# Six small moves in a one-core hybrid layer: where loads, copies and splits of weights stand in their queues

## The chip, the cores and the metric

The kernel runs on one core of one Trainium2 chip. The metric is the device time of one execution in microseconds (us), as the median of several. A profiled execution is a further one, with its own time; its span runs from the first to the last instruction.

A core has five engines, each with its own queue that is worked through in order: TensorE (PE; its weight loads are shown as PEld), VectorE (DVE), ScalarE (ACT), GpSimd (POOL) and SyncE (SP), which here only issues transfers (DMA). ScalarE issues some transfers too.

## The reference

One layer of a language model for 512 tokens of 1024 numbers, all in float32. In outline:

```python
h = rms_norm(x, norm_mix_pre)
z = h @ w_in                                   # 1024 -> 8016
o_a = rwkv7_time_mix(z[:, :3360], ...)         # 16 heads of 64, state recurrence, group norm, gate g = sigmoid(gd) @ g2
o_b = nsa_attention(z[:, 3360:5968], ...)      # 16 query heads in 4 groups: compressed, selected, window branch
g_a, g_b = split(sigmoid(z[:, 5968:]), 2)
m = g_a * (o_a @ w_branch_rwkv) + g_b * (o_b @ w_branch_nsa)
x = x + rms_norm(m @ w_out, norm_mix_post)
u = causal_dwconv(rms_norm(x, norm_ffn_pre) @ ffn_up, conv_w, conv_b)   # 1024 -> 2 x 2816
x = x + rms_norm((silu(u_gate) * u_val) @ ffn_down, norm_ffn_post)
```

With 512 tokens there are eight blocks of 64 keys and up to 16 may be selected, so the selected branch takes every block that is allowed. The window of 512 covers the whole sequence as well.

## The kernel before, in words

**Products in two halves.** To keep float32 accuracy on TensorE's reduced float32 format, each operand is split into a high part (a copy in that format) and a low part (what is left). A product is three matmuls: high with high, high with low, low with high (`mm3`, `proj_steps`). Activations are split once. Weights are split as they come: `split_to` loads a raw tile by SP, copies it to the high part on ScalarE (`act`, L124) and subtracts on GpSimd or VectorE for the low part (L162). `split_w` does so for the two halves of a block of 1024 x 128 weights. Raw, high and low tiles each stand in a ring of three buffers (`WB = 3`, tags `raw`, `whi`, `wlo`), so a load waits until a raw tile three loads back is split.

**Stages.** (1) Norm of x, transposed into `hh`, `hl`; low-rank projections. (2) RWKV in two groups of four head pairs: `inputs` projects k, r, v of a pair, `prep` computes decays and normalised keys, `couple` makes the chunk matrices, `invert` and `recur` solve and run the recurrence over eight chunks of 64, and `finish` normalises the group's output, adds the bonus (`bvl`), multiplies by the gate and writes to DRAM. (3) Attention in eight phases, one for each pair of heads p8: in a phase `values(p8)` (transposes and products with values) and `score(p8 + 1)` (scores, softmax) are woven together with projection work as filling. (4) The two branch projections and gates (`branch`). (5) The output projection by token tiles of 128 (`wo_tok`), residual and norm. (6) The gated MLP: `half_up` for the first `NU = 3` blocks of up-weights by halves of the tokens, then 41 whole blocks; (7) the down projection.

**What sets the order.** The code is written as Python generators. `drive` runs one filling generator and, in each round, advances the spawned threads by their rate (`FR = 0.5`: a step every second round). In the attention phases `steps` sorts the steps of all generators by a fraction of the phase. This gives the program order. A planner then lists the instructions anew: on each engine it takes, among those that by its own timing are ready, the first in program order. So an instruction that is ready early floats ahead, and one edit can reorder what follows. `tc.keep_in_program_order(i)` pins an instruction behind all that was traced before it on its engine; `late=True` does so for the high copy of a split. The order on an engine is then fixed, and the engine waits for whatever stands first.

**What the change touches.**

- `finish` (L824): for each pair it splits its gate weights g2 (L847), loads `bvl` (L850), and three steps later transposes the output to a bank `gt` of tag `px`, scales it, adds `bvl` (L866), and multiplies by the gate product `pg` (also `px`; L871 to L875). The first group's finish runs beside `prep` and `couple` of the second group, the second group's beside the attention's first phases.
- PSUM banks: tags `pj`, `px`, `py`, `pz`, two each. `prep` puts the squared norms of the keys into `pn` (L533), from which ScalarE (L536) and then GpSimd (`nte`, L544) make the factors that `pb`'s transposes (L562) need.
- `invert` has a scratch tile `TM` in pool `rh` (L642).
- `vcp` (L988 to L993): the compressed values, masked and split, on ScalarE and VectorE ahead of the attention; the first values phase reads them at L1154. `vload` (L996) loads and transposes the other values as a thread of its own.
- `qload` (L929) loads the four half tiles of a pair's queries; called at the start of phase p8 for pair p8 + 2.
- `norm` in `score` (L1051): scales the softmax numerators of both branches, on VectorE for branch b = 0 and on GpSimd for b = 1, but on VectorE for both in the first head of the first pair (L1061).
- `wo_load` (L1263): loads and splits output weights during the branch stage; the first `NW = 13` go to tiles of their own.
- The stretch between output projection and MLP (L1413 to L1426): `norm_x` and `norm_t` of token tiles 2 and 3 beside `half_up`.

## Time and profile before

| | |
|---|---|
| median of 3 runs | 1175.86 us (1175.56, 1175.86, 1177.87) |
| profiled execution, its own time | 1178.1 us |
| its span | 1176.3 us |
| TensorE busy | 1153.3 us, 98% of the span |
| VectorE, ScalarE, GpSimd busy | 580.7, 579.6, 581.4 us |
| mean clock granted to TensorE | 0.993 |
| transfers | 131.94 MB, mean 112 GB/s |

How to read it. A row of busy time by stage has the stretch in us from the span's start, its length, and for each engine its busy us with the number of instructions; then the clock granted to TensorE (1.00 is full), the share of the transfer engines and GB/s. A row of a timeline has start, duration, engine, line, operation, `out<-in`, shapes, and in brackets how long the engine stood before it and what ended that. A row of waits has the total in us, how often, and the longest. Matmuls are pipelined and their ends are modelled: on their own they are 0.39 us long in the timeline, though one starts about every 0.23 us.

### The profile page before, as it was taken

To read this page: it belongs to the slowest core of one execution; us is meant where nothing else is said; L and a number is where in the kernel's file an instruction comes from. 1 tells how busy PE (TensorE), PEld (TensorE's weight loads), DVE (VectorE), ACT (ScalarE), POOL (GpSimd) and SP (SyncE) were. 2 spreads that over 40 slices of the span, in tenths; PEclk is the share of its full clock that TensorE was granted. 3 is DMA by queue.
4 is the path that set the end of the run, shared out by engine and by line. 5 is a ranking of instruction groups with operands and counts; after the bars stand their busy time and mean duration, and the time that the engine had idled before them with its cause. 6 is when DMAs were issued, how large, how long until landed. Compare 5 with 4: busy or idle time off the path is not lost.

```text
span 1176.3 us, 19883 instructions
## 1 busy us (share of the span) xinstructions
PE 1153.3 (98%) x7414; PEld 923.4 (78%) x7414; DVE 580.7 (49%) x1208; ACT 579.6 (49%) x1149; POOL 581.4 (49%) x525
## 2 busy tenths in 40 slices
PE   8999999999999999999999999999999999999997
PEld 6888888877788887766767777788888888888886
DVE  4225555635555552678887757655433343331103
ACT  5536653544665434467776655443544444443311
POOL 4336664435576442456576553511555565554430
PEclk8999999999999999989999999999999999999999
DMA  6522335321343653233533126541223233334421
GB/s 226 133 81 74 88 101 169 108 82 42 107 140 100 190 178 122 78 99 125 178 105 95 54 64 210 180 160 45 72 90 101 97 99 99 98 92 138 129 63 72
DMA packets 95651, 131.94 MB, mean 112 GB/s; under 512 B 34178, under 2 KB 37058, under 8 KB 95299
## 3 DMA queue, kind: packets, MB, share of 16 engines
q1 hardware_dynamic: 79634, 116.26, 31.7%
q10 hardware_dynamic: 15920, 14.42, 3.9%
q8 instruction: 58, 0.95, 0.3%
q14 instruction: 39, 0.31, 0.1%
HBM read 108.30 MB, written 19.14 MB: 108 GB/s over the span
## 4 chain that ended last, share of the span: by engine, by line
PE 86%; DVE 5%; issue 3%; ACT 2%; POOL 2%; DMA 1%; SPq 0%; DVEq 0%; POOLq 0%; ACTq 0%
PE pu L222 6%; PE pu L221 6%; PE pu L223 6%; PE o L1134 4%; PE dn L1307 3%; PE dn L1308 3%; PE dn L1309 3%; PE pt L140 3%; PE gt L299 2%; PE gt L301 2%; PE gt L300 2%; PE ub L1191 2%; PE v L300 2%; PE v L299 2%; PE s L1078 2%
## 5 line engine op out<-in xcount | busy, mean ns | idle before, releaser
L1087 ACT ACTIVATE p<-p,stt 128x384 f32<-128x384 f32 (+3 forms) x128 | 70.7, 554 | 40.7 <-DVE stt L1085 39.3
L1449 DVE SCALAR_TENSOR_TENSOR u<-pu,cvec,u 128x511 f32<-128x511 f32 x44 | 33.0, 750 | 102.0 <-ACT u L1448 102.0
L1061 POOL TENSOR_SCALAR p<-p,stt 128x512 f32<-128x512 f32 (+3 forms) x60 | 68.4, 1151 | 26.7 <-DVE stt L1056 19.8
L1085 DVE CUSTOM_DVE_ANT_0 p<-s,rh 128x384 f32<-128x384 f32 (+3 forms) x128 | 59.3, 483 | 26.6 <-PE s L1071 17.8
L1453 POOL TENSOR_TENSOR u<-u,u 128x512 f32<-128x512 f32 x22 | 28.4, 1292 | 39.1 <-DVE u L1450 38.2
L140 PE MATMUL pt<-ident,p 128*128 128x128 f32 x320 | 45.5, 276 | 1.5 <-POOL p L1061 0.8
L1455 DVE TENSOR_TENSOR al<-u,ah 128x512 fp32r<-128x512 f32 x22 | 23.8, 1081 | 45.5 <-ACT ah L1454 45.5
L1134 PE MATMUL o<-PT,vt 128*64 128x256 f32 (+3 forms) x256 | 46.2, 452 | 0.0
L140 PEld LDWEIGHTS pt<-ident,p 128*128 128x128 f32 x320 | 38.0, 142 | 8.0 <-ACT p L1087 1.1
L1078 PE MATMUL s<-kst,qs 128*128 128x512 f32 (+1 forms) x128 | 38.4, 391 | 2.0 <-DVE stt L1085 2.0
L1448 ACT ACTIVATE u<-pu,cvec 128x512 f32<-128x512 f32 x44 | 33.6, 763 | 5.5 <-PE pu L1411 5.5
L1061 DVE TENSOR_SCALAR p<-p,stt 128x512 f32<-128x512 f32 (+3 forms) x68 | 35.4, 553 | 0.6
L1450 DVE SCALAR_TENSOR_TENSOR u<-pu,cvec,u 128x510 f32<-128x510 f32 x44 | 33.0, 749 | 1.6
L1134 PEld LDWEIGHTS o<-PT,vt 128*64 128x64 f32 x256 | 17.3, 139 | 19.6 <-issue 17.6
L1125 ACT ACTIVATE PT<-pt 128x512 f32<-128x512 f32 x48 | 27.5, 585 | 5.7 <-PE pt L140 5.6
L1078 PEld LDWEIGHTS s<-kst,qs 128*128 128x128 f32 x128 | 21.6, 191 | 10.9 <-DVE stt L1085 6.3
L1355 DVE TENSOR_TENSOR p2tm<-dn,gb 128x512 f32<-128x512 f32 x4 | 2.8, 692 | 51.2 <-ACT p2jl L1353 51.2
L1127 DVE COPY PT<-pt 128x512 f32<-128x512 f32 x32 | 21.9, 684 | 9.1 <-PE pt L140 9.0
L1454 ACT ACTIVATE ah<-u 128x512 fp32r<-128x512 f32 x22 | 13.9, 633 | 22.4 <-POOL u L1453 22.4
L804 ACT ACTIVATE UV<-xs 64x256 f32<-64x256 f32 x16 | 6.0, 378 | 37.5 <-PE xs L799 37.1
L1087 ACT ACTIVATION_READ_ACCUMULATOR p<-p,stt 128x1 f32 x128 | 24.1, 188 | 0.0
L657 DVE TENSOR_TENSOR XP<-XP,TM 128x30 f32<-128x30 f32 (+14 forms) x60 | 20.3, 338 | 2.0
(1758 smaller groups left out, 3943.9 us busy)
## 6 DMA issues: line engine op xcount, KB each, us to landing
gtd<-gt ACTq DMA_DIRECT2D x16, 256.0 KB, 2.6
qs<-qd SPq DMA_DIRECT2D x32, 128.0 KB, 3.1
g<-gtd SPq DMA_DIRECT2D x16, 256.0 KB, 3.3
xt<-in_x_dram SPq DMA_DIRECT2D x4, 512.0 KB, 4.7
bvd<-bv SPq DMA_DIRECT2D x8, 256.0 KB, 2.2
bvl<-bvd SPq DMA_DIRECT2D x8, 256.0 KB, 2.7
oad<-y SPq DMA_DIRECT2D x8, 256.0 KB, 2.5
kst<-kst ACTq DMA_DIRECT2D x16, 128.0 KB, 2.9
```

Source lines behind the costliest of these rows:

```text
L140: return te.transpose(o, i, ident)
L221: te.matmul(p, wh(k), mh(k), start=first and k == 0, stop=False)
L222: te.matmul(p, wh(k), ml(k), start=False, stop=False)
L223: te.matmul(p, wl(k), mh(k), start=False, stop=last and k == n - 1)
L299: te.matmul(p, wh(k), hh[:, k, :], start=k == 0, stop=False)
L300: te.matmul(p, wh(k), hl[:, k, :], start=False, stop=False)
L1061: (po if b and (p8 or e) else ve).tensor_scalar(o.pe[e, b, k], o.pe[e, b, k], st[e][:, 3, i:i + 1], None, op0=OP.mult)
L1078: m = te.matmul(s_[:, :n], qt, kt[:, x, b, :n], start=x == 0, stop=x == 1)
L1085: ve.tensor_tensor_reduce(sb, parts[b], rh[e][:, (3 - qb) * 128:], -1.0, BIG, OP.add, OP.min, st[e][:, 0, i:i + 1])
L1087: sc.activation(sb, sb, AF.Exp, scale=-1.0, bias=st[e][:, 0, i:i + 1], accum_out=st[e][:, 1, i:i + 1])
L1134: te.matmul(acc[e * 64:e * 64 + 64, j * 128:], vt[:, j, b * 256 + g * 64:b * 256 + g * 64 + 64], m[e][:, c:c + n], start=False, stop=k == ...
L1307: te.matmul(acc[half, t], sh[:, k, tsl], wh[kk], start=k == 0, stop=False)
```

## The change

It has these parts:

1. In `finish` the raw tile of g2 no longer comes from the ring of weights: it takes the place of `TM` in pool `rh` (one buffer; `TM` grows from 240 to 256 columns to fit). `bvl` is loaded one step later and pinned on SP's queue.
2. `pn` takes a bank of tag `py` in place of `px`.
3. `vcp` is made at the end of `vload` instead of ahead of the attention.
4. The query loads are pinned on SP's queue, and in phase p8 they are traced at 0.55 of the phase by a generator of their own.
5. The first head's scaling for branch b = 1 goes to GpSimd like all others.
6. The high copies of the first 13 output weights, and of up-block 3, are pinned; up-block 3's split is written ahead of the MLP loop.
7. `norm_t` of token tile 2 is written behind both `half_up(0, 0)` and `half_up(1, 0)`.

```diff
--- before.py
+++ after.py
@@ -153,20 +153,20 @@
     eps6 = vec[:, V_EPS:V_EPS + 1]
     epsg = vec[:, V_EPS + 1:V_EPS + 2]
 
-    def split_to(src, hi, lo, name, n, eng=None, p=None, late=False):
-        raw = (p or wp).tile([128, n], F32, tag="raw", name=name + "r", bufs=WB)
+    def split_to(src, hi, lo, name, n, eng=None, p=None, late=False, tag="raw", bufs=WB):
+        raw = (p or wp).tile([128, n], F32, tag=tag, name=name + "r", bufs=bufs)
         sy.dma_start(raw, src)
         i = act(hi, raw, AF.Copy)
         if late:
             tc.keep_in_program_order(i)
         (eng or po).tensor_tensor(lo, raw, hi.bitcast(F32), op=OP.subtract)
 
-    def split_w(src, name):
+    def split_w(src, name, late=False):
         hs, ls = [], []
         for i in range(2):
             hi = wp.tile([128, 512], F32R, tag="whi", name=f"{name}h{i}", bufs=WB)
             lw = wp.tile([128, 512], F32R, tag="wlo", name=f"{name}l{i}", bufs=WB)
-            split_to(src[:, i * 512:i * 512 + 512], hi, lw, f"{name}{i}", 512)
+            split_to(src[:, i * 512:i * 512 + 512], hi, lw, f"{name}{i}", 512, late=late)
             hs.append(hi)
             ls.append(lw)
         return hs, ls
@@ -529,7 +529,7 @@
         F = rw.tile([128, S], F32, tag="T", name=f"F{p}", bufs=NT)
         sc.activation(F, pa, AF.Identity, scale=hka[:, p:p + 1], bias=oka[:, p:p + 1])
         yield
-        pn = (pz if p == GP else px)(f"pn{p}")
+        pn = (pz if p == GP else py)(f"pn{p}")
         for t in range(4):
             te.matmul(pn[:, 2 * t:2 * t + 2], Q[:, t * 128:(t + 1) * 128], sel, start=True, stop=True)
         nt = rw.tile([128, 8], F32, tag="nt", name=f"nt{p}", bufs=2)
@@ -639,7 +639,7 @@
     def invert(gr, g):
         XL = rh_.tile([128, 2, 32, 32], F32, tag="XB", name=f"XL{g}", bufs=2)
         LU, XU = XL[:, 0], XL[:, 1]
-        TM = rh_.tile([128, 240], F32, tag="TM", name=f"TM{g}", bufs=1)
+        TM = rh_.tile([128, 256], F32, tag="TM", name=f"TM{g}", bufs=1)
         for h in range(2):
             for b in range(2):
                 sy.dma_start(LU[64 * h + 32 * b:64 * h + 32 * b + 32], gr.ld[b, :, :, h].rearrange("p c i t -> (p c) i t"))
@@ -844,11 +844,11 @@
                 ahead.append(scaled(i + 2))
             gh = rh_.tile([128, 256], F32R, tag="gh", name=f"gh{p}", bufs=1)
             gl = rh_.tile([128, 256], F32R, tag="gl", name=f"gl{p}", bufs=1)
-            split_to(a["g2"][p], gh, gl, f"g2{p}", 256, late=True)
+            split_to(a["g2"][p], gh, gl, f"g2{p}", 256, p=rh_, late=True, tag="TM", bufs=1)
             po.tensor_copy(gh[64:96, 128:], gl[64:96, 128:].bitcast(F32))
+            yield
             bvl = rh_.tile([128, S], F32, tag="bvl", name=f"bvl{p}", bufs=1)
-            sy.dma_start(bvl, bvd[p])
-            yield
+            tc.keep_in_program_order(sy.dma_start(bvl, bvd[p]))
             yield
             yield
             pt = px(f"gt{p}")
@@ -931,7 +931,8 @@
         for e in range(2):
             q = nk.tile([128, S], F32R, tag="qs", name=f"qs{p8}{e}", bufs=4)
             for x in range(2):
-                sy.dma_start(q[(e ^ x) * 64:(e ^ x) * 64 + 64].bitcast(F32), qd[p8, x, e * 64:e * 64 + 64])
+                tc.keep_in_program_order(sy.dma_start(q[(e ^ x) * 64:(e ^ x) * 64 + 64].bitcast(F32),
+                                                      qd[p8, x, e * 64:e * 64 + 64]))
             qs[p8].append(q)
 
     def queries(p8):
@@ -986,11 +987,6 @@
     vt = na.tile([128, 4, 512], F32, name="vt")
     kst += [na.tile([128, 2, 2, S], F32R, name=f"kst{g}") for g in (2, 3)]
     vcp = na.tile([128, 4, 2, 128], F32R, name="vcp")
-    for e in range(2):
-        m = vec[:, V_SEL + e:V_SEL + e + 1]
-        ec = slice(e * 64, e * 64 + 64)
-        sc.activation(vcp[:, :, 0, ec], vcc, AF.Copy, scale=m)
-        ve.scalar_tensor_tensor(vcp[:, :, 1, ec], vcc, m, vcp[:, :, 0, ec].bitcast(F32), op0=OP.mult, op1=OP.subtract)
     nw = pool("nw", "left", nctx)
     zp = nw, "PT", 6
     def vload():
@@ -1005,6 +1001,12 @@
                 tr(pt[:, t * 128:(t + 1) * 128], z[:, t * 128:(t + 1) * 128], ident)
             sc.activation(vt[:, :, b * 128:(b + 1) * 128], pt.rearrange("p (t f) -> p t f", f=128), AF.Copy)
             yield
+        for e in range(2):
+            m = vec[:, V_SEL + e:V_SEL + e + 1]
+            ec = slice(e * 64, e * 64 + 64)
+            sc.activation(vcp[:, :, 0, ec], vcc, AF.Copy, scale=m)
+            ve.scalar_tensor_tensor(vcp[:, :, 1, ec], vcc, m, vcp[:, :, 0, ec].bitcast(F32), op0=OP.mult, op1=OP.subtract)
+        yield
 
     def compressed(p8, o):
         g = p8 // 2
@@ -1058,7 +1060,7 @@
                                  op=OP.mult)
             for b in range(2):
                 i = b * 4 + k
-                (po if b and (p8 or e) else ve).tensor_scalar(o.pe[e, b, k], o.pe[e, b, k], st[e][:, 3, i:i + 1], None, op0=OP.mult)
+                (po if b else ve).tensor_scalar(o.pe[e, b, k], o.pe[e, b, k], st[e][:, 3, i:i + 1], None, op0=OP.mult)
 
         done = []
         for e, qb in ((0, 3), (0, 2), (1, 3), (1, 2), (0, 1), (0, 0), (1, 1), (1, 0)):
@@ -1218,12 +1220,12 @@
     for p8 in range(8):
         v = values(p8, os_[p8])
         s = score(p8 + 1, os_[p8 + 1]) if p8 < 7 else iter(())
-        if p8 < 6:
-            qload(p8 + 2)
+        qn = queries(p8 + 2) if p8 < 6 else iter(())
 
         def steps():
             n = FILL2[p8]
             order = [((i + 0.1) / 5, v) for i in range(5)] + [((i + 0.3) / 8, s) for i in range(8)]
+            order += [(0.55, qn)]
             if p8 == PX:
                 order += [(0.3, fill)]
                 order += [(0.05 * (i + 0.5), rest) for i in range(9)] + [(0.05 * (i + 1.5), load) for i in range(9)]
@@ -1267,7 +1269,7 @@
             hi, lo = (mp.tile([128, 512], F32R, name=f"wo{x}{i}") for x in "hl")
         else:
             hi, lo = (wp.tile([128, 512], F32R, tag=f"w{x}", name=f"wo{x}{i}", bufs=WB) for x in ("hi", "lo"))
-        split_to(a["wo"][half, q][:, kk * 512:kk * 512 + 512], hi, lo, f"wok{i}", 512, ve if i < NW else po, p)
+        split_to(a["wo"][half, q][:, kk * 512:kk * 512 + 512], hi, lo, f"wok{i}", 512, ve if i < NW else po, p, late=i < NW)
         wo_w[half, k] = hi, lo
 
     with pool("bp", "left") as bp:
@@ -1418,12 +1420,12 @@
             norm_t(xn[t - 1], t - 1, h2h, h2l, "n2")
         xn[t] = norm_x(x2[:, t, :], t, [g2b[:, 0:512], g2b[:, 512:]], "n2", op)
     pu4 = [py("pu0"), py("pu1"), pj("pu2")]
-    half_up(0, 0)
+    for b in range(NU - 1):
+        half_up(b, 0)
     norm_t(xn[2], 2, h2h, h2l, "n2")
-    for b in range(1, NU - 1):
-        half_up(b, 0)
     norm_t(xn[3], 3, h2h, h2l, "n2")
     half_up(NU - 1, 0)
+    after = {NU: split_w(a["up"][NU], f"up{NU}", True)}
     octx.close()
     bctx.close()
     dump("x2", x2.rearrange("p a b -> p (a b)"))
@@ -1440,7 +1442,7 @@
                     p = pu4[blk]
                     half_up(blk, 1)
                 else:
-                    wh, wl = split_w(a["up"][blk], f"up{blk}")
+                    wh, wl = after.get(blk) or split_w(a["up"][blk], f"up{blk}")
                     p = pj(f"pu{blk}")
                     mm3(p, wslice(wh), wslice(wl), lambda k: h2h[:, k, :], lambda k: h2l[:, k, :])
                 cv = blk * 4
```

## The prediction

> **What bounds the kernel now.** I read the page first (busy time and the chain that ended last), then TensorE's waits, then busy time by stage, then single instructions around each stage in which TensorE stands.

> ```profile
> span 1176.3 us, 19883 instructions
> PE 1153.3 (98%) x7414; PEld 923.4 (78%) x7414; DVE 580.7 (49%) x1208; ACT 579.6 (49%) x1149; POOL 581.4 (49%) x525
> PE 86%; DVE 5%; issue 3%; ACT 2%; POOL 2%; DMA 1%; SPq 0%; DVEq 0%; POOLq 0%; ACTq 0%
> ```

> TensorE is busy for 1153.3 of 1176.3 us, and the other three for half of it. The change neither adds nor removes a matmul, so it can only win from the 1176.3 - 1153.3 = 23.0 us in which TensorE stands, and from time in which its clock is low. Busy time by stage says where these are (columns: stretch, its length, busy us of PE, PEld, DVE, ACT, POOL, then the granted clock):

> ```profile
> 300.00:335.00 35.00, 31.77 (x206) 25.63 (x205) 18.30 (x25) 20.77 (x36) 24.06 (x25) 1.00 0.39 118
> 493.00:497.00 4.00, 3.08 (x18) 2.35 (x17) 3.74 (x11) 2.34 (x5) 3.26 (x4) 1.00 0.65 221
> 504.00:521.00 17.00, 14.13 (x69) 9.53 (x69) 13.78 (x49) 9.91 (x32) 7.88 (x10) 0.90 0.45 139
> 725.00:746.00 21.00, 20.18 (x87) 15.71 (x86) 15.10 (x20) 11.04 (x20) 8.28 (x6) 1.00 0.64 215
> 808.00:816.00 8.00, 6.80 (x58) 6.54 (x58) 5.85 (x11) 3.74 (x10) 1.69 (x2) 1.00 0.54 166
> ```

> Length minus PE busy gives the idle time: 3.23, 0.92, 2.87, 0.82 and 1.20 us in the five, 9.04 together. An edit reaches each of the five; the other 14.0 us lie at the kernel's start, at its end and in small pieces, and no edit is aimed there. TensorE's three longest waits behind the start name their releasers (total, times, longest):

> ```profile
> PE r L301 <- POOL r6l L162: 1.5, 1, 1.5
> PE pg L871 <- ACT nt L536: 1.2, 1, 1.2
> PE n2p L140 <- DVE n2xn L198: 1.2, 1, 1.2
> ```

> The third stage also has a lower clock, 0.90. Cut at the clock's own steps, it looks like this:

> ```profile
> 510.69:514.11 3.42, 2.67 (x13) 1.79 (x11) 0.61 (x3) 0.15 (x1) 1.52 (x2) 1.00 0.34 86
> 514.11:517.53 3.42, 2.31 (x16) 1.82 (x16) 3.26 (x11) 3.42 (x12) 1.79 (x2) 1.00 0.46 146
> 517.53:520.94 3.41, 2.88 (x9) 1.43 (x9) 3.35 (x11) 0.09 (x1) 1.54 (x4) 0.50 0.63 199
> 520.94:524.36 3.42, 3.42 (x15) 2.09 (x12) 1.40 (x5) 1.45 (x3) 3.26 (x4) 0.50 0.00 1
> ```

> After two stretches in which TensorE is busy for 78% and 68%, it gets half its clock for 6.83 us. It is busy for 2.88 + 3.42 = 6.30 us of them, which full clock does in 3.15.

> **Which time the sum is made against.** The profiled execution took 1178.1 us, 2.24 above the median of 1175.86; its span is 1176.3, with 1.8 around it. The three unprofiled times lie at 1175.56, 1175.86 and 1177.87, so two are about 2.4 below the profiled one. A half-clock stretch that the profiled execution had and those two had not would cost 3.15 less the waits it covers. That is an inference. I make the sum of waits against 1178.1 and take the same sum off the median.

> **A. Own raw tile for g2, and the pn bank (L157, L532, L847).** The finish's g2 load takes one of three raw buffers (WB) that all weight blocks go through, and keeps it until its split, which is pinned on ScalarE:

> ```profile
> 303.39 0.33 SPq L158 DMA_DIRECT2D g22r<-in_g_dram  x1
> 305.89 0.33 SPq L158 DMA_DIRECT2D r60r<-in_wf_dram  x1
> 308.96 0.63 ACT L124 ACTIVATE r6h<-r60r 128x512 fp32r<-128x512 f32 x1 [2.20 <-DMA r60r<-in_wf_dram]
> 324.62 0.94 POOL L162 TENSOR_TENSOR gl<-g22r,gh 128x256 fp32r<-128x256 f32 x1 [1.90 <-ACT gh L124]
> ```

> g22r holds its buffer from 303.39 to 325.56, 22 us. Without it r60r is issued at 303.39 or before, 2.5 us earlier, which covers the 2.20 ScalarE stood for it; the weights behind follow. I take the whole 1.5 of r6l (bounds 0 and 1.5). The bank of pn is the second wait: pg needs a bank of tag px, and ScalarE frees pn's only after a table load.

> ```profile
> 313.45 0.18 ACT L536 ACTIVATE nt<-pn 128x8 f32<-128x8 f32 x1
> 313.68 0.50 PE L871 MATMUL pg<-lg1h,gh 128*128 128x512 f32 x1 [1.23 <-ACT nt L536]
> 314.13 0.61 POOL L544 COPY nte<-nt 128x512 f32<-128x512 f32 x1 [1.83 <-DVE nt L538]
> ```

> In tag py pg need not wait, but next in TensorE's queue stand pb's transposes (L562), which need nte, done at 314.74: they start right behind pg now. If ScalarE's chain stays where it is, pb waits instead and the gain is 0. The chain follows r6h, which comes 2.2 us sooner, more than the 1.23. I take 0.9 of 1.23 (bounds 0 and 1.23). The rest of this stage, 3.23 - 1.5 - 1.23 = 0.5, is another px bank's: nothing. **A: -2.4**, bounds -3.2 and 0.

> The bias load bvl moves behind one yield and is pinned on SP's queue, so y2's addition (L866) and the weights' low halves queued behind it on POOL would wait if it came late:

> ```profile
> 304.64 0.33 SPq L850 DMA_DIRECT2D bvl<-bvd  x1
> 318.04 1.75 POOL L866 TENSOR_TENSOR y<-y,bvl 128x512 f32<-128x512 f32 x1
> ```

> It is read 13.4 us after its issue; one yield at rate FR = 0.5 is two rounds of the driver, each of them three projection matmuls and what the other threads add, a few us. Nothing.

> **B. Value copies behind the value loads (L989 to L993).**

> ```profile
> 492.65 0.82 DVE L993 SCALAR_TENSOR_TENSOR vcp<-vcc,vec,vcp 128x256 fp32r<-128x256 f32 x1
> 493.89 0.47 DVE L993 SCALAR_TENSOR_TENSOR vcp<-vcc,vec,vcp 128x256 fp32r<-128x256 f32 x1
> 494.68 0.68 DVE L1085 CUSTOM_DVE_ANT_0 p<-s,rh 128x512 f32<-128x512 f32 x1
> ```

> They cost VectorE 1.29 us right ahead of the first score's reduction, for which TensorE stands 0.92. Behind the last value copy they meet a VectorE that is waiting for TensorE in the stretch 510.69 to 514.11 (0.61 of 3.42 busy). **B: -0.9**, bounds -0.92 and 0.

> **C. First scores' scaling, and queries (L1061, L932, L1222).** For the first head pair's first head, the scaling of branch b = 1 goes from VectorE to POOL: four instructions.

> ```profile
> 508.19 3.40 POOL L1061 TENSOR_SCALAR p<-p,stt 128x512 f32<-128x512 f32 x2 [3.67 <-DVE stt L1056]
> 515.62 3.02 DVE L1061 TENSOR_SCALAR p<-p,stt 128x256 f32<-128x256 f32 x4
> 518.67 0.68 DVE L1108 TENSOR_TENSOR pct<-pct,pct 64x512 fp32r<-64x512 f32 x1
> ```

> POOL has 3.67 us free ahead of its own pair, and VectorE sheds two of the four that delay pct by 3.02 us: half of it, 1.5. With g2 out of the raw ring, q7's and ksp's weights also come sooner and TensorE has more to fill with. Against it, the other waits of this stage have their own causes. **C: -1.5** of 2.87, bounds -2.87 and the price of the rival below.

> [...]

> The query loads move from a phase's start to its middle:

> ```profile
> 588.13 6.49 SPq L934 DMA_DIRECT2D qs<-qd  x4
> 621.56 1.08 PE L1015 MATMUL pc<-kcs,qs 128*128 128x64 f32 x8
> 645.40 1.08 PE L1015 MATMUL pc<-kcs,qs 128*128 128x64 f32 x8
> ```

> They are read 33 us after the issue, and a phase takes 23.8 (621.56 to 645.40); 0.55 of one later, 20 are left. Nothing, unless SP is held for that long.

> **D. Output-weight splits pinned (L1270).**

> ```profile
> 729.51 0.63 ACT L124 ACTIVATE woh<-wok6r 128x512 fp32r<-128x512 f32 x1 [1.87 <-DMA wok6r<-in_wo_dram]
> 730.05 0.62 ACT L124 ACTIVATE wb13h<-wb130r 128x512 fp32r<-128x512 f32 x1
> ```

> ScalarE stands 1.87 us for a weight that isn't needed before the next stage, with wb13h queued behind it, and TensorE waits in this stage, for wb13l's low half. Pinned, it falls behind. **D: -0.6** of 0.82, bounds -0.82 and +0.6 (the order wrong by one such split).

> **E. Third token tile's norm moved, up3 pinned (L1421 to L1427).**

> ```profile
> 805.19 0.63 ACT L124 ACTIVATE up3h<-up30r 128x512 fp32r<-128x512 f32 x1 [3.38 <-issue]
> 812.61 0.69 DVE L212 TENSOR_TENSOR hl<-n2p,hh 128x512 fp32r<-128x512 f32 x1 [0.33 <-ACT hh L124]
> 813.41 1.42 DVE L198 SCALAR_TENSOR_TENSOR n2xn<-x,n2r,gb 128x512 f32<-128x512 f32 x2
> ```

> The third tile's hl stands ahead of the fourth's n2xn; moved behind half_up(1,0) it doesn't. But both tiles' transposes share two pz banks, so the fourth's then wait for that same hl. TensorE has half_up(2,0) to fill with. I take half of 1.20: **E: -0.6**, bounds -1.20 and +0.7 (one hl more).

> **Sum.** -2.4 - 0.9 - 1.5 - 0.6 - 0.6 = -6.0. The planner orders anew behind every edit, and the traced order has small waits of its own wherever its timing was off; I allow two of the size of the 0.5 left in A, 1.0. So -5.0: 1178.1 - 5.0 = 1173.1 with the half-clock stretch, 2.24 less without, and **1175.86 - 5.0 = 1170.9** by the median. Its own range is 1168.5 to 1173.4.

> **Rivals.** *The waits only move* (0.21). [...]

> *A longer lull at the attention's start: slower* (0.13). POOL runs in order. If the first head's two scalings (b = 1, 512 and 384 wide) are queued ahead of the second head's but aren't done by 508.19, the pair that ends in TensorE's wait for p is late by up to both:

> ```profile
> L1061 POOL TENSOR_SCALAR p<-p,stt 128x512 f32<-128x512 f32 (+3 forms) x60 | 68.4, 1151 | 26.7 <-DVE stt L1056 19.8
> ```

> That is 2 x 1.15 = 2.3, to 3.4 at the pair's own pace. Two more stretches under 78% then bring a second half-clock stretch, 3.15. Without C the other parts give -4.5 + 1.0, so 1178.1 - 3.5 + 2.3 to 3.4 + 3.15 = 1180.1 to 1181.2 with both stretches, 1177.8 to 1178.9 with one fewer. It decides from a start of the scalings after 505.9 (508.19 - 2.3). Against it: the 3.67 us that POOL stood free.

> [...]

> *More than the sum* (0.10). If C's whole 2.87 and D's and E's waits go, -2.4 - 0.9 - 2.87 - 0.82 - 1.2 = -8.2: 1167.7.

> **How the numbers follow.** The forecast has 0.56. A measurement here can tell about 0.2% from no change, 2.35 us: faster is below 1173.5. Faster has the forecast, the larger gain and 0.01 of the first rival: 0.67; same the other 0.20 of that and 0.01 of the second: 0.21; slower 0.12. The range reaches from the larger gain with a little beyond it, 1167.0, to 1177.0, which leaves out most of the slower rival.

> **What would show it.** In the changed trace: r60r and r61r issued before g22r's split; no wait of pg for nt, nor of pb for nte; TensorE's idle time in the five stages down from 9.0 to about 4; no half-clock stretch near the first values, or a shorter wait ahead of it; woh never between two wb splits; n2p's wait for n2xn halved. Wrong would be: these waits gone and the time unchanged, which needs new ones of the same sum; or the scaling on POOL as the last releaser ahead of TensorE.

## The result, and the profile after

The changed kernel takes 1171.66 us (median of five, 1171.09 to 1172.26), beside 1175.86 us for the kernel before (five, 1175.56 to 1179.63). The ratio is 0.9947 [0.9932, 0.9962], a gain of 6.2 us with 4.5 to 8.0 as its interval: faster by more than the 0.2% that can be told from no change. The two medians of five lie 4.2 us apart; the 6.2 goes by the ratio on record, which isn't the ratio of these medians. The forecast was 1170.9, in a range from 1167.0 to 1177.0. Run again on another chip, the changed kernel gave 0.9948 [0.9935, 0.996].

The profiled execution took 1171.09 us, 7.0 less than the one before (1178.1). Two lines of its page (span; busy time by engine):

```profile
span 1169.3 us, 19893 instructions
PE 1149.0 (98%) x7414; PEld 923.0 (79%) x7414; DVE 577.4 (49%) x1204; ACT 580.2 (50%) x1149; POOL 588.0 (50%) x529
```

TensorE's idle time fell from 23.0 to 20.3 us and its busy time from 1153.3 to 1149.0, though the matmuls are the same 7414: a 512 wide one at half clock is busy for 0.63 us in the changed kernel and one starts every 0.43 (510.53 to 513.09), for 0.39 and 0.23 at full clock, and there are fewer of them (3.41 us of half clock in the attention, for 6.83). Busy time by stage of the changed kernel, over the same five stages (each stretch starts about 3 to 6.5 us earlier here):

```profile
297.00:332.00 35.00, 34.22 (x218) 28.01 (x217) 18.57 (x27) 23.03 (x39) 26.41 (x27) 1.00 0.41 124
490.00:494.00 4.00, 3.58 (x19) 2.38 (x17) 4.00 (x12) 2.44 (x7) 3.51 (x4) 1.00 0.73 240
501.00:518.00 17.00, 12.89 (x64) 10.10 (x62) 11.41 (x36) 9.95 (x32) 11.65 (x14) 0.90 0.21 70
722.00:743.00 21.00, 21.00 (x94) 17.42 (x93) 15.62 (x20) 10.45 (x20) 11.65 (x8) 1.00 0.74 235
801.50:809.50 8.00, 8.00 (x70) 7.86 (x69) 5.37 (x11) 3.65 (x11) 0.00 (x0) 1.00 0.01 2
```

Idle time is now 0.78, 0.42, 4.11, 0 and 0 us (before: 3.23, 0.92, 2.87, 0.82 and 1.20). Four stages gained; the third, the attention's start, lost 1.24. TensorE's waits say what is late there (total, times, longest):

```profile
PE s L1080 <- DVE stt L1087: 3.1, 8, 1.2
...
PE pt L140 <- POOL p L1063: 2.4, 1, 2.4
...
PE pg L871 <- DVE stt L1057: 1.5, 1, 1.5
PE r L301 <- POOL r6l L162: 0.6, 1, 0.6
```

The waits of pg for nt and of n2p for n2xn are gone, and r6l's fell from 1.5 to 0.6. In their place stand one for p, whose last releaser is GpSimd's scaling, and one behind VectorE's factors of the softmax (`stt`).

**A measure that does not depend on idle time.** Since both kernels issue the same matmuls, each one can be found in both traces by its operands and its count. How much earlier it starts in the changed kernel is that kernel's lead there, and the growth of the lead over a stage is what the stage gained. These are medians of lead differences, worked out from the two traces; the stages are named after the forecast's terms. The lead at the kernel's start differs by up to 2.0 us between executions, though no edit reaches it, so totals of single profiles are not compared below, only stages. The starts are of two kinds: in before, after, c_after, u_vcp and n_mix TensorE starts 9 or 10 matmuls between 6 and 9 us, and their leads at 285 us lie within 0.32; in the others it starts 4 (7 in u_up), and they are 1.0 to 1.7 us behind the changed kernel's first profile.

| gain over a stage, us | A (285 to 340) | B and C (470 to 560) | D (690 to 755) | E (755 to 830) |
|---|---|---|---|---|
| before to after | +2.80 | +0.35 | +2.32 | +1.32 |
| after to c_after (same program) | -0.02 | +0.14 | +0.01 | 0.00 |
| after to u_g2 | **-2.71** | +1.23 | 0.00 | +0.02 |
| after to u_pn | **-1.02** | +0.12 | 0.00 | +0.06 |
| after to u_norm | -0.30 | **+2.31** | +0.01 | +0.02 |
| after to u_vcp | +0.16 | **-0.94** | 0.00 | +0.02 |
| after to u_query | -0.76 | **-0.06** | +0.01 | 0.00 |
| after to u_attn | +0.39 | **+2.37** | 0.00 | +0.02 |
| after to n_ve | +0.33 | **+2.83** | 0.00 | +0.06 |
| after to n_mix | -0.85 | **+3.88** | 0.00 | +0.06 |
| after to u_wo | +0.29 | +0.53 | **-1.60** | 0.00 |
| after to u_n2 | -0.96 | +0.12 | 0.00 | **-0.42** |
| after to u_up | -0.22 | +1.52 | 0.00 | **-0.81** |

Bold is the stage that the experiment edits. The plain numbers tell how far a stage moves by itself: by nothing in D and E, by up to about 1 us in A, and by up to 1.5 in B and C. The experiments below explain most of the last two.

### The profile page after: what moved, and what is told of

The parts are those of the page before. It is cut to its first block, busy times and chain, and to the rows that moved or that the text cites. A ratio compares the mean times of both kernels' runs of the same rounds, so it can differ in the third digit from the quotient of the medians.

```text
span 1169.3 us, 19893 instructions
## 1 busy us (share of the span) xinstructions
PE 1149.0 (98%) x7414; PEld 923.0 (79%) x7414; DVE 577.4 (49%) x1204; ACT 580.2 (50%) x1149; POOL 588.0 (50%) x529
## 4 chain that ended last, share of the span: by engine, by line
PE 91%; DVE 4%; ACT 2%; POOL 1%; issue 1%; DMA 0%; SPq 0%; DVEq 0%; POOLq 0%; ACTq 0%
PE pu L221 6%; PE pu L223 6%; PE pu L222 6%; PE o L1136 3%; PE dn L1311 3%; PE dn L1310 3%; PE dn L1309 3%; PE pt L140 3%; PE ub L1193 3%; PE ub L1195 2%; PE ub L1194 2%; PE gt L299 2%; PE gt L301 2%; PE gt L300 2%; PE v L300 2%; PE v L299 2%
## 5 line engine op out<-in xcount | busy, mean ns | idle before, releaser
L1063 POOL TENSOR_SCALAR p<-p,stt 128x512 f32<-128x512 f32 (+1 forms) x64 | 73.2, 1154 | 23.8 <-DVE stt L1058 17.1
L140 PE MATMUL pt<-ident,p 128*128 128x128 f32 x320 | 44.4, 273 | 2.5 <-POOL p L1063 2.4
L1457 DVE TENSOR_TENSOR al<-u,ah 128x512 fp32r<-128x512 f32 x22 | 23.8, 1080 | 45.4 <-ACT ah L1456 45.4
L140 PEld LDWEIGHTS pt<-ident,p 128*128 128x128 f32 x320 | 37.7, 141 | 7.2 <-POOL p L1063 2.6
L1063 DVE TENSOR_SCALAR p<-p,stt 128x512 f32<-128x512 f32 (+1 forms) x64 | 32.8, 544 | 0.8
L657 DVE TENSOR_TENSOR XP<-XP,TM 128x30 f32<-128x30 f32 (+14 forms) x60 | 20.3, 338 | 2.0
```

The lines of the kernel that those rows point to most:

```text
L140: return te.transpose(o, i, ident)
L1063: (po if b else ve).tensor_scalar(o.pe[e, b, k], o.pe[e, b, k], st[e][:, 3, i:i + 1], None, op0=OP.mult)
```

## The experiments

Each kernel is the changed one with one edit; a name with u_ undoes a part, n_ is a new version, c_after is the changed kernel itself. A diff's minus line is the changed kernel's. Ratios are against the kernel before on the same chip.

**u_g2: g2's raw tile back in the ring of weights.**

```diff
-split_to(a["g2"][p], gh, gl, f"g2{p}", 256, p=rh_, late=True, tag="TM", bufs=1)
+split_to(a["g2"][p], gh, gl, f"g2{p}", 256, late=True)
```

> The changed kernel with g2 again in the ring of raw weight tiles. Theory 1 (part A as recorded: the ring delays r6's weights and ScalarE's chain behind them): r6l's wait of 1.5 us comes back, and pb waits for nte about 1 us though pn keeps its new bank; the lead of 2.8 us that the changed kernel won between 300 and 340 us falls to about 0.4, the time rises by 2.4 us. Rival (the bank of pn alone did it): less than 1 us lost there.

Measured: 1175.11 us, 0.9975 [0.9966, 0.9985], against 1172.44 for c_after on the same chip: 2.67 us lost, and 2.71 in stage A. Two waits of TensorE and four single instructions of this kernel:

```profile
PE r L301 <- POOL r6l L162: 1.5, 1, 1.5
...
PE pb L140 <- POOL nte L544: 1.4, 1, 1.4
```

```profile
306.95 0.33 SPq L158 DMA_DIRECT2D r60r<-in_wf_dram  x1
310.05 0.63 ACT L124 ACTIVATE r6h<-r60r 128x512 fp32r<-128x512 f32 x1 [2.15 <-DMA r60r<-in_wf_dram]
313.43 0.40 PE L871 MATMUL pg<-lg1h,gh 128*128 128x512 f32 x1
315.89 0.66 PE L140 MATMUL pb<-ident,nte 128*128 128x128 f32 x4 [1.37 <-POOL nte L544]
```

With pn in tag py, pg stands for nothing, as planned; but ScalarE again stands 2.15 us for r60r, nt comes late, and pb behind pg takes over the wait. The same instructions in the changed kernel:

```profile
299.72 0.33 SPq L158 DMA_DIRECT2D r60r<-in_wf_dram  x1
305.92 0.63 ACT L124 ACTIVATE r6h<-r60r 128x512 fp32r<-128x512 f32 x1 [1.33 <-PE v L300]
312.31 0.40 PE L871 MATMUL pg<-lg1h,gh 128*128 128x512 f32 x1
313.25 0.60 PE L140 MATMUL pb<-ident,nte 128*128 128x128 f32 x4
319.08 0.50 PE L301 MATMUL r<-hh,r6l 128*128 128x512 f32 x1 [0.65 <-POOL r6l L162]
```

All of A comes from the raw tile.

**u_pn: pn back in tag px.**

```diff
-        pn = (pz if p == GP else py)(f"pn{p}")
+        pn = (pz if p == GP else px)(f"pn{p}")
```

> The changed kernel with pn back in a bank of tag px; g2 keeps its own tile. Theory 1 (part A as recorded: with ScalarE's chain 2 us sooner the bank is worth 0.9 us): pg waits for nt again, TensorE's lead between 300 and 340 us falls by 0.9 and the time rises as much. Rival (with the chain sooner pn is read before pg needs its bank, so the bank's move is worth nothing): the lead there stays within 0.3 us.

Measured: 1171.37 us, 0.9937 [0.9921, 0.9953], no slower than the changed kernel's 0.9947. nt is done 1.1 us before pg starts, and pg doesn't wait:

```profile
312.32 0.18 ACT L536 ACTIVATE nt<-pn 128x8 f32<-128x8 f32 x1
...
313.64 0.40 PE L871 MATMUL pg<-lg1h,gh 128*128 128x512 f32 x1
314.58 0.60 PE L140 MATMUL pb<-ident,nte 128*128 128x128 f32 x4
```

Once ScalarE's chain is early the bank is free in time in either tag, so on top of the raw tile the bank move is worth nothing. The -1.02 in stage A arises 14 us later, in a wait of pg for gh (L848) of 0.9, and u_n2, u_query and n_mix have the same 0.9 although their code there is the changed kernel's. It follows the landing of one weight tile, lw6r, in u_n2 and in the changed kernel:

```profile
320.74 0.33 SPq L158 DMA_DIRECT2D lw6r<-in_lwa_dram  x1
324.87 0.42 ACT L124 ACTIVATE lh<-lw6r 128x256 fp32r<-128x256 f32 x1 [2.05 <-DMA lw6r<-in_lwa_dram]
```

```profile
319.06 0.33 SPq L158 DMA_DIRECT2D lw6r<-in_lwa_dram  x1
322.22 0.42 ACT L124 ACTIVATE lh<-lw6r 128x256 fp32r<-128x256 f32 x1 [1.08 <-DMA lw6r<-in_lwa_dram]
```

From issue to use it is 4.13 us there and 3.16 here, and 3.9 to 4.1 in the other three. g2's split stands behind lh on ScalarE and GpSimd. Why that transfer takes a microsecond longer in some executions is open.

**u_norm: the first head's scaling of branch b = 1 back on VectorE.**

```diff
-(po if b else ve).tensor_scalar(o.pe[e, b, k], o.pe[e, b, k], st[e][:, 3, i:i + 1], None, op0=OP.mult)
+(po if b and (p8 or e) else ve).tensor_scalar(o.pe[e, b, k], o.pe[e, b, k], st[e][:, 3, i:i + 1], None, op0=OP.mult)
```

> The changed kernel with the first head's scaling for branch 1 back on VectorE. Theory 1 (the recorded sum: this move won 1.5 us): the time rises from 1171.7 to about 1173.2 us. Theory 2 (the slower rival's first half: POOL's two extra scalings stand ahead of the second head's pair and make it late, the wait of pt for p being 2.41 us now against 0.75 before): that wait falls back below 1 us, and the time falls by about 1.7 us to 1170.0; if the half-clock stretch behind the wait goes too, another 1.7 us, 1168.3.

Measured: 1169.93 us, 0.9924 [0.991, 0.9937], 2.7 us better than the changed kernel by the ratios, 2.31 in the stage. What the move to GpSimd did is seen in the changed kernel's own rows, GpSimd's first and then TensorE's:

```profile
502.69 2.84 POOL L1063 TENSOR_SCALAR p<-p,stt 128x512 f32<-128x512 f32 x2
505.62 0.62 POOL L1049 TENSOR_SCALAR rh<-dist 128x512 f32<-128x512 f32 x1
506.33 3.26 POOL L1063 TENSOR_SCALAR p<-p,stt 128x512 f32<-128x512 f32 x2
509.64 0.44 PE L140 MATMUL pt<-ident,p 128*128 128x128 f32 x2 [2.41 <-POOL p L1063]
```

In the kernel before this wait was 0.75:

```profile
511.65 0.44 PE L140 MATMUL pt<-ident,p 128*128 128x128 f32 x2 [0.75 <-POOL p L1061]
```

The first head's two scalings hold GpSimd from 502.69 to 505.53, the second head's pair starts right behind at 506.33, and TensorE stands for its end. Cut close to the clock's own steps, the changed kernel shows what follows:

```profile
506.88:510.29 3.41, 1.00 (x8) 0.72 (x6) 0.06 (x1) 0.88 (x4) 2.70 (x2) 0.98 0.50 156
510.29:513.70 3.41, 3.41 (x11) 2.73 (x10) 1.38 (x5) 1.51 (x5) 0.00 (x0) 0.52 0.21 77
```

TensorE is busy for 1.00 of 3.41 us and then gets half its clock for 3.41. u_norm has no such stretch here. Its wait for p is 1.77, not below 1 as expected, so only 0.64 of the growth from 0.75 to 2.41 goes away with the move.

**n_ve: both heads of the first pair on VectorE.** 
```diff
-(po if b else ve).tensor_scalar(o.pe[e, b, k], o.pe[e, b, k], st[e][:, 3, i:i + 1], None, op0=OP.mult)
+(po if b and p8 else ve).tensor_scalar(o.pe[e, b, k], o.pe[e, b, k], st[e][:, 3, i:i + 1], None, op0=OP.mult)
```

> The changed kernel with all scaling of the first head pair on VectorE, the second head's branch 1 as well. Theory 2 (POOL's late pair ends TensorE's longest wait of this stage, 2.41 us, and the low clock follows from it): that wait goes, no half-clock stretch, 1171.7 - 2.4 - 1.7 = about 1167.6 us where the changed kernel takes 1171.7, and about 1 us less than with the first head alone on VectorE. Theory 3 (VectorE is the limit of this stage): four more scalings of 0.3 to 0.4 us push its later work back, and it's no better than with the first head alone, or worse.

Measured: 1169.75 us, 0.9927 [0.9915, 0.9939], 2.69 less than c_after on the same chip; +2.83 in the stage, no half clock. TensorE no longer stands for GpSimd, but a new wait comes some 8 us later, since VectorE is now the late one:

```profile
518.59 0.63 PE L140 MATMUL gt<-ident,YT 128*128 128x128 f32 x4 [1.61 <-DVE sc L1024]
```

**n_mix: between the two.** VectorE takes the whole first head and the widest scaling of the second head.

```diff
-(po if b else ve).tensor_scalar(o.pe[e, b, k], o.pe[e, b, k], st[e][:, 3, i:i + 1], None, op0=OP.mult)
+(po if b and (p8 or (e and k < 3)) else ve).tensor_scalar(o.pe[e, b, k], o.pe[e, b, k], st[e][:, 3, i:i + 1], None, op0=OP.mult)
```

> The changed kernel with the first head's scaling and the widest one of the second head on VectorE, the second head's other three for branch 1 on POOL. If POOL's pair is what TensorE waits for, and VectorE the limit once it does all of it (with all eight there TensorE waits 1.6 us for VectorE's compressed scores instead), this has less of both waits than either neighbour: a ratio to the kernel before of 0.992 or less, against 0.9948 for the changed kernel, 0.9924 with the first head on VectorE and 0.9927 with both. If the low clock alone made the difference, it equals the two, 0.9925 within 0.0012.

Measured: 1167.84 us, 0.9905 [0.9889, 0.992], the lowest ratio of all kernels here, about 5 us below the changed kernel; its interval still meets those of u_norm and n_ve. Neither of the two waits is left at size:

```profile
505.24 2.06 DVE L1063 TENSOR_SCALAR p<-p,stt 128x512 f32<-128x512 f32 x3
505.79 1.29 POOL L1063 TENSOR_SCALAR p<-p,stt 128x384 f32<-128x384 f32 x1
...
507.35 0.66 PE L140 MATMUL pt<-ident,p 128*128 128x128 f32 x4 [0.25 <-DVE p L1063]
```

**u_vcp: the value copies back ahead of the attention.** The loop stands right behind the making of `vcp` again, and no longer ends `vload`.

```diff
     vcp = na.tile([128, 4, 2, 128], F32R, name="vcp")
+    for e in range(2):
...
+        sc.activation(vcp[:, :, 0, ec], vcc, AF.Copy, scale=m)
+        ve.scalar_tensor_tensor(vcp[:, :, 1, ec], vcc, m, vcp[:, :, 0, ec].bitcast(F32), op0=OP.mult, op1=OP.subtract)
```

> The changed kernel with the value copies back ahead of the attention. Theory 1 (the recorded sum): the 0.92 us wait of the first scores for VectorE comes back, 1171.7 + 0.9 = 1172.6 us. Theory 2 (in their new place the copies hold VectorE just as long, 0.9 us at 502.79, ahead of the scores' last reductions, which TensorE's 1.49 us wait of pg ends on): the wait at the first score comes back but that of pg gets shorter, and the time stays within 0.5 us of 1171.7.

Measured: 1173.42 us, 0.9954 [0.9941, 0.9966]. The half-clock stretch is the same 3.41 us as in the changed kernel, so the stage's -0.94 is the copies'. TensorE's wait at the first scores is back (0.87, against 0.27 in the changed kernel), and pg's wait of 1.5 is gone. This is the place of the first copy in u_vcp:

```profile
489.81 0.84 DVE L994 SCALAR_TENSOR_TENSOR vcp<-vcc,vec,vcp 128x256 fp32r<-128x256 f32 x1
```

**u_query: queries loaded at a phase's start, not pinned.** The loads in `qload` lose their pins as well.

```diff
-        qn = queries(p8 + 2) if p8 < 6 else iter(())
+        if p8 < 6:
+            qload(p8 + 2)
...
-            order += [(0.55, qn)]
```

> The changed kernel with the query loads back at the start of a phase, not pinned. Theory 1 (the recorded sum: the move costs and brings nothing, the loads being read 20 us later): within 0.5 us of 1171.7. Theory 2: the loads' place in SP's queue shifts other loads; then the 1.25 us wait of the second phase's first scores, which the changed kernel has and the one before had not, goes away, and the time falls to about 1170.5 us.

Measured: 1173.6 us, 0.9949 [0.9936, 0.9962]; -0.06 in its stage. Its -0.76 in stage A is lw6r's landing again. The wait of the second phase's first scores stays, at 1.28.

**u_attn: the three attention edits undone together**, by the diffs of u_norm, u_vcp and u_query.

> The changed kernel with the scaling, the value copies and the query loads all as before; the raw tile, the bank of pn, the output weights and the norm stay changed. Theory 1 (the recorded sum, 0.9 + 1.5 of it from these): 1171.7 + 2.4 = 1174.1 us. Theory 2 (the three together won nothing; between 480 and 560 us the changed kernel's lead grew by 0.36 us only, with half the half-clock time of the profile before): within 0.7 us of 1171.7.

Measured: 1170.69 us, 0.9933 [0.9921, 0.9945]; +2.37, which neither theory had. TensorE's waits are again those of the kernel before, but for the first, which was 0.5 there:

```profile
PE o L1154 <- DVE pct L1108: 1.1, 1, 1.1
PE pt L140 <- POOL p L1061: 0.8, 1, 0.8
```

But this profile has no half clock in the attention, where the kernel before had 6.83 us of it. With that code the stage is 0.35 + 2.37 = 2.72 us faster than in the kernel before, close to the 3.15 that the forecast put on the stretch. So the stretch comes or not with the same attention code.

**u_wo: output-weight splits not pinned.** 
```diff
-split_to(a["wo"][half, q][:, kk * 512:kk * 512 + 512], hi, lo, f"wok{i}", 512, ve if i < NW else po, p, late=i < NW)
+split_to(a["wo"][half, q][:, kk * 512:kk * 512 + 512], hi, lo, f"wok{i}", 512, ve if i < NW else po, p)
```

> The changed kernel with the output-weight splits not pinned. Theory 1 (part D as recorded, from the 0.82 us that TensorE stood in this stage): the time rises by 0.6 us. Rival (the stage won more than its idle time showed: TensorE's lead grew by 2.3 us between 705 and 748 us): the time rises by 2.3 us, all of it there.

Measured: 1174.27 us, 0.9972 [0.9962, 0.9982], 1.83 more than c_after on the same chip; -1.60 in stage D. ScalarE stands for an output weight with wb14h queued behind it, as in the kernel before:

```profile
736.02 0.63 ACT L124 ACTIVATE woh<-wok11r 128x512 fp32r<-128x512 f32 x1 [1.13 <-DMA wok11r<-in_wo_dram]
736.56 0.61 ACT L124 ACTIVATE wb14h<-wb141r 128x512 fp32r<-128x512 f32 x1
...
737.63 0.39 PE L1194 MATMUL ub<-sp,wb14h 128*128 128x512 f32 x1
738.59 0.50 PE L1195 MATMUL ub<-sp,wb14l 128*128 128x512 f32 x1 [0.57 <-POOL wb14l L162]
```

The bracket says 0.57, but from start to start it is 0.96 where these matmuls follow each other every 0.23: 0.73 are lost. The idle time is counted from the modelled end of the matmul before, 0.39 us after its start.

**u_n2: the third tile's transposes back between the half blocks.** 
```diff
-    for b in range(NU - 1):
-        half_up(b, 0)
+    half_up(0, 0)
     norm_t(xn[2], 2, h2h, h2l, "n2")
+    for b in range(1, NU - 1):
+        half_up(b, 0)
```

> The changed kernel with the third tile's transposes back ahead of half_up(1, 0); the pinned split of up-block 3 stays. Theory 1 (part E as recorded, half of the 1.20 us wait, from the order of the transposes): the wait of n2p for n2xn comes back and 0.6 to 1.3 us are lost between 800 and 820 us (1.27 is what the lead grew there). Rival (the two up-block splits that stood on ScalarE ahead of the fourth tile's squares were the cause): less than 0.3 us lost.

Measured: 1172.66 us, 0.9945 [0.9931, 0.9959]; -0.42 in stage E. The wait of n2p for n2xn is back at 0.3, where the kernel before had 1.2.

**u_up: up-block 3's split back in the loop, not pinned.** 
```diff
-    after = {NU: split_w(a["up"][NU], f"up{NU}", True)}
...
-                    wh, wl = after.get(blk) or split_w(a["up"][blk], f"up{blk}")
+                    wh, wl = split_w(a["up"][blk], f"up{blk}")
```

> The changed kernel with up-block 3's split not pinned and back in the loop; the transposes keep their new order. Theory 1 (the order of the transposes made part E): less than 0.3 us lost between 800 and 820 us. Rival (the splits ahead of the fourth tile's squares on ScalarE, 1.3 us for two of them): up to 1.3 us lost there.

Measured: 1173.13 us, 0.9948 [0.9931, 0.9964]; -0.27 near 778 and -0.54 behind 800, more than the first theory's 0.3, with a wait that the changed kernel doesn't have:

```profile
809.44 0.66 PE L140 MATMUL n2p<-ident,n2xn 128*128 128x128 f32 x4 [0.45 <-DVE hl L212]
```

**c_after: the changed kernel again**, beside u_g2, u_wo and n_ve.

> The changed kernel once more, beside the others of this chip: its ratio to the kernel before should be 0.9947 within 0.0015, as in the first comparison. The half-clock stretch at 510 us should show again if the wait ahead of it is its cause.

Measured: 1172.44 us, 0.9948 [0.9935, 0.996]. The half-clock stretch is there again, from 510.0 to 513.4, and no stage moved by more than 0.14.

## Why the prediction was right, step by step

The size was forecast at 5.0 and came out at 6.2 [4.5, 8.0] by the ratio. The stages of the profiled pair add up to 2.80 + 0.35 + 2.32 + 1.32 = 6.8. The terms behind this did not come out alike, and that they add up so well is in part luck:

| term | forecast gain | measured | by |
|---|---|---|---|
| A | 2.4 | 2.8 | before to after; u_g2 -2.71 |
| B | 0.9 | 0.94 beside C, about 0 without it | u_vcp; u_norm less u_attn |
| C | 1.5 | a loss of 2.3, about 0.9 of it without the half clock | u_norm; u_g2 and u_up |
| D | 0.6 | 2.3, of it 1.6 by the pin | before to after; u_wo |
| E | 0.6 | 1.3 | before to after; u_n2 0.42, u_up 0.81 |
| allowance | -1.0 | nothing outside the stage of B and C | stages |

**A** held as a sum, not in its parts. That r60r comes earlier, and ScalarE's chain with it, is what happened: it was issued 6.2 us earlier (299.72 for 305.89) where at least 2.5 were forecast, and split 3.0 earlier. But "the whole 1.5 of r6l" was 0.87, since the wait did not vanish, and "0.9 of 1.23" for pn's bank was 1.6 and belongs to the raw tile: without the tile pb takes over the wait, which the text named as its condition for 0, and without the bank move nothing is lost. The other 0.3 came later in the stage.

**B** came out at its size, but only beside C. The copies do stand ahead of the first scores, and moving them takes that wait from 0.92 to 0.27. Yet u_norm, which has the moved copies (and the query move, worth nothing) but not C, is no faster in the stage than u_attn, which has none of them (2.31 and 2.37, both without half clock): there the waits only move, to pg (1.0 for 0.4) and to p (1.8 for 0.8). The forecast took the parts as independent, and these two are not. Each number is from one profile.

**C** has the wrong sign. The step that failed is "POOL has 3.67 us free ahead of its own pair". The row was right for the kernel before, but the change itself shortened this time. The first two rows are of the kernel before, the other two of the changed one: the end of GpSimd's work ahead, and the factor (`stt`) that releases its pair:

```profile
504.24 0.28 POOL L848 CAST gh<-gl 32x128 fp32r<-32x128 f32 x1
507.82 0.17 DVE L1056 TENSOR_TENSOR stt<-stt,gates 128x4 f32<-128x4 f32 x1
```

```profile
502.15 0.44 POOL L848 CAST gh<-gl 32x128 fp32r<-32x128 f32 x1
504.24 0.17 DVE L1058 TENSOR_TENSOR stt<-stt,gates 128x4 f32<-128x4 f32 x1
```

GpSimd is done with gh 1.9 us earlier (504.52 and 502.59), but the factor comes 3.6 earlier (507.99 and 504.41), which leaves 1.8 us of 3.5. The two scalings that moved there take 2.84. Behind them, and now ahead of the pair, stands a mask step of 0.62, which followed the pair before (at 511.68). So the pair starts at 506.33, 1.9 us behind its factor, where it was 0.2 before. In the time of before (3.6 later) the scalings start at 506.3, past the 505.9 that the text named as the point that decides. Without them, in u_norm, the pair's end comes about 1.0 us earlier against the rest of TensorE's work.

That is the "longer lull", to which the forecast gave 0.13: its mechanism came, at less than the 2.3 to 3.4 that it named for GpSimd's part, and A, D and E outweighed it. Of the half clock, one stretch less came than before, not one more. Two kernels with the changed kernel's attention code, u_g2 and u_up, have none in it, and gained 1.23 and 1.52 there: an estimate of the price of one stretch from these two is about 1.4. Taken out of u_norm's 2.31, it leaves 0.9 for the order on GpSimd. The stage as a whole won 0.35 from before to after. About 1.4 of that is the half of the half-clock time that went away, so B and C together lost about 1.0, where a gain of 2.4 was forecast. VectorE needed no relief: with all scalings on it (n_ve) the first transposes stand for none of them (those of p start at 506.65, without a wait).

**D** was mis-sized because "length minus PE busy" counts too little. Single matmuls of the kernel before in stage D:

```profile
741.11 0.39 PE L1192 MATMUL ub<-sp,wb14h 128*128 128x512 f32 x1
741.42 0.50 PE L1193 MATMUL ub<-sp,wb14l 128*128 128x512 f32 x1
...
744.05 0.39 PE L1192 MATMUL ub<-sp,wb15h 128*128 128x512 f32 x1
744.60 0.50 PE L1193 MATMUL ub<-sp,wb15l 128*128 128x512 f32 x1 [0.16 <-POOL wb15l L162]
```

The first pair is 0.31 apart, not 0.23, with no wait in the record; the second 0.55 with a wait of 0.16, so 0.32 were lost. The first matmul behind a wait is also 0.11 longer. Between 717 and 749 us such places add up to 2.2 us in the kernel before, where the forecast had 0.82 of idle time. The changed kernel has none of them there: its matmuls run every 0.23 us. But the copies did not fall behind, as the forecast had it. They still stand between two weight splits, now where their transfers have landed, so that ScalarE doesn't wait for any:

```profile
726.13 0.62 ACT L124 ACTIVATE woh<-wok2r 128x512 fp32r<-128x512 f32 x1
...
727.17 0.61 ACT L124 ACTIVATE wb13h<-wb131r 128x512 fp32r<-128x512 f32 x1
```

Without the pin (u_wo) 1.6 are lost; the order there isn't that of the kernel before, and which edit brought the other 0.7 is open.

**E** was mis-sized by "I take half of 1.20": 1.32 went. u_n2 and u_up give 0.42 and 0.81 of it, 1.23. So the larger part came with the split of up-block 3, for which the forecast had no price; it had put all of E on the order of the transposes. These did not stand for the third tile's hl, which the text had feared.

**Queries, bvl and the rest at nothing**: u_query bears the first out (-0.06); bvl was not tried by itself.

**Of the signs named**, r60r and r61r are issued ahead of g22r (the first at 299.72, g22r at 306.29), pg and pb stand for nothing, and n2p's wait is gone. But woh still stands between two wb splits. Idle time in the five stages fell from 9.0 to 5.3, not to about 4; the third stage has 1.2 more than before. The wait ahead of the half-clock stretch was to be shorter and is longer, and the scaling on GpSimd is the last releaser ahead of TensorE, which the text had named as the sign of its being wrong.

**The inference on the spread** is not borne out. If the half-clock stretch made some executions of the kernel before 2.4 us longer, time and clock would go together. On another chip, executions of it with a mean clock of 0.999 took 1180.15 and 1178.07 us, and with 0.995 they took 1179.24 and 1180.85. The test is weak, since the mean holds the kernel's start too: u_attn, which starts 4 matmuls between 6 and 9 us, is given a clock of 1.00 up to 15 us, and the changed kernel, which starts 10, is given 0.50 from 9 to 15 us. What spreads the times is open.

So the total was right, but partly by luck: C's loss was met by D and E, which won 2.4 more than forecast, by the allowance, which was not used, and by half of the half-clock time, which went away.

## What to carry to other kernels

Free time of an engine ahead of an instruction is not fixed room for more work: both of its ends move with the change. The rows to read are what ends the work ahead, what releases the instruction behind, how far the same change shifts each of them, and what else in the in-order queue will then stand between (here GpSimd's mask step of 0.62 us). Parts that meet at one engine need not add up: undo them singly and together. A load that holds a shared buffer for long is worth more to free than the wait that it shows, since the chain behind it moves as a whole: 2.71 us by u_g2, where r6l's wait was 1.5. Where matmuls overlap, count lost time from start to start against the steady step, since short waits vanish in the modelled ends: two matmuls started 0.31 us apart, for 0.23, with no wait in the record.

## What the runs showed of the hardware

**The same scaling on two engines.** A 512 and a 384 wide one take GpSimd 2.84 to 3.26 us in the changed kernel. On VectorE in n_ve four of them take 1.78:

```profile
505.38 1.78 DVE L1063 TENSOR_SCALAR p<-p,stt 128x512 f32<-128x512 f32 x4
```

In the kernel before two 512 wide ones on VectorE take 0.87 together (at 504.59) while GpSimd stands, and one takes 0.92 (at 508.24) beside GpSimd's pair: VectorE is slowed there, while the records of the two engines overlap.
